# Normed input in two steps and one more block pair: a feed-forward change in a macaron block

## The chip, the cores and the metric

The kernel runs on one core of one Trainium2 chip. The metric is the device time of one execution in microseconds (us), the median of several runs. All times below are microseconds unless marked ns.

## The reference, cut to what matters

One layer: a half-weighted feed-forward network, a token mixer with two kinds of attention, a second half-weighted feed-forward network, and a last norm. There are 512 tokens of width 1024; the inner width of the feed-forward networks is 2816. All data are float32.

```python
def rmsnorm(x, g):
    y = x32 * lax.rsqrt(jnp.mean(x32 * x32, axis=-1, keepdims=True) + EPS)
    return (y * g.astype(jnp.float32)).astype(x.dtype)

def swiglu(x, w_gate, w_up, w_down):
    return (jax.nn.silu(x @ w_gate) * (x @ w_up)) @ w_down

x = x + 0.5 * swiglu(rmsnorm(x, ffn1_norm), ffn1_w_gate, ffn1_w_up, ffn1_w_down)
x = x + token_mixer(rmsnorm(x, mix_norm), ...)
x = x + 0.5 * swiglu(rmsnorm(x, ffn2_norm), ffn2_w_gate, ffn2_w_up, ffn2_w_down)
return rmsnorm(x, final_norm)
```

## The kernel before

Everything is held transposed: the width lies on the 128 partitions, so x is eight tiles `x[k]` of 128 x 512 (k = 0 to 7), and the inner width 2816 is 22 tiles j. [...] One product is three matmuls (`mm3`): high by high, high weight by low input, low weight by high input, at lines 98, 99 and 100. ScalarE makes the high part by a copy and VectorE the low part by a subtraction; for weights this is `split_w` (lines 89 and 90), on halves of a tile that the DMA queue of SP brings in, 512 KB each, three buffers deep (`raw`, `wh`, `wl`).

`ffn` runs once for each feed-forward network, with the names' suffix a or b; the text calls them layer one and layer two. It goes through the 22 tiles in three parts.

Plain tiles, j below `N0` = 6. Gate and up products use `eh` and `el`, the input times the norm's gain, but without the root mean square, which isn't known yet. 48 matmuls of 512 columns make a tile. While they run, `means` takes the column sums of the squares `sq` with four small matmuls and a chain of small VectorE operations (`rsqrt_steps`), and `spread` makes the factor `bc` for all partitions with one matmul and a copy into `rbc`. `hooks` says after which (j, k) each is called. `gate` then multiplies both results by `bc`, takes the Silu and the product, and `activated` splits the result into `ah` and `al` for the down projection: three multiplications and a subtraction on VectorE. In layer one the first two tiles are made together with the loading of x, so that its loop starts with j = 2.

Block pairs, j from 6 on, two tiles at a time, `pair`. The gate products of two tiles are made with seven block products instead of eight (Winograd's form of Strassen's scheme): on the weights' side with sums of weight blocks (`s1`, `s2`, and a difference in place of `raw`), on the input's side with four combinations t0 to t3 of the halves of two input tiles. This needs the normed input itself: `xh` and `xl`, and the combinations split as `th` and `tl`. The seven products are 84 matmuls of 256 columns; the two up products are plain, 24 matmuls of 512 columns each, and come after the gate products. The combinations of partial sums are taken out of PSUM between the products.

`normed(p)`, p = 0 to 3, prepares two input tiles each: the normed tiles `nx`, their parts `xh` and `xl`, the four combinations in two work tiles, and eight splits of 256 columns. It is called after (3, 3), (3, 7), (4, 3) and (4, 7).

Down projection: eight output tiles, 66 matmuls each.

TensorE's order is the order of the program (a manual schedule). The orders of VectorE and ScalarE in `ffn` are made by the scheduler of the language, from its own estimates, and are fixed in the program; each engine works them off in order, with semaphores between the engines. A weight split that stands behind other work on VectorE waits for it. PSUM has four banks for tiles of tag `mm` (plain tiles and pairs' gate products) and two of tag `t` (the pairs' up products). Work tiles of tags `ob` and `ptb` have two buffers each, and `slot` names 512-column places, in which the 22 tiles `ah` take slots 0 to 21.

Of the kernel before, what the change touches and what calls it, by code (L numbers as in the profile page):

```python
# [13 lines left out]
F32 = mybir.dt.float32  # L14
# [6 lines left out]
P = 128  # L21
# [14 lines left out]
WARM = 7  # L36
DIRECT = (0, 7)

N0 = 6
HS = S // 2  # L40
F32_MAX = 3.4028234e38
PSUM = bass.MemoryType.PSUM
# [5 lines left out]
def tile_macaron(ctx: ExitStack, tc, xs, xT, wf, wgu1, wst1, wd1, wqk, wv, wo, wgu2, wst2, wd2,  # L48
# [121 lines left out]

        return means, spread

    def ffn(wgu, wst, wd, norm, early, res, nm, hooks, first=None, last_halves=None):

# [1 line left out]

        eh, el = early
        ah, al, due = [None] * JF, [None] * JF, []  # L180
        th, tl = [], []

        def activated(j, t):
            h = ah[j] = slot(j, f"ah{nm}{j}", F32R)
# [2 lines left out]
            V.tensor_tensor(l[:], t[:], h[:].bitcast(F32), op=ALU.subtract)  # L187

        def gate(j, pg, pu):
            bc = res["bc"]  # L190
            t1 = tp.tile([P, S], F32, tag="ptb", name=f"t1{nm}{j}")
            V.tensor_tensor(t1[:], pg[:], bc[:], op=ALU.mult)
            A.activation(t1[:], t1[:], AF.Silu)
            t2 = tp.tile([P, S], F32, tag="ob", name=f"t2{nm}{j}")
            V.tensor_tensor(t2[:], pu[:], bc[:], op=ALU.mult)
            V.tensor_tensor(t2[:], t2[:], t1[:], op=ALU.mult)
            activated(j, t2)

        def t_tiles():
            tp.tile([P, 8], F32, tag="odd", name=f"odd{nm}", bufs=1)  # L200
            tiles = [tp.tile([P, 1280], F32R, tag=f"pr{i % 2}", name=f"tt{nm}{i}")
                     for i in range(4)]
            more = tp.tile([P, 12 * HS], F32R, tag="tx", name=f"tx{nm}", bufs=1)
            places = [t[:, i * HS:(i + 1) * HS] for t in tiles for i in range(5)]
            places += [more[:, i * HS:(i + 1) * HS] for i in range(12)]
            th.extend(places[4 * p:4 * p + 4] for p in range(4))
            tl.extend(places[16 + 4 * p:20 + 4 * p] for p in range(4))

        def normed(p):

            b = []
            for k in (2 * p, 2 * p + 1):
                t = tp.tile([P, S], F32, tag="ob", name=f"nx{nm}{k}")
                V.scalar_tensor_tensor(t[:], x[k], gain(norm, k), res["bc"][:],
                                       op0=ALU.mult, op1=ALU.mult)
                A.copy(xh[k][:], t[:])
                V.tensor_tensor(xl[k][:], t[:], xh[k][:].bitcast(F32), op=ALU.subtract)
                b += [t[:, :HS], t[:, HS:]]
            ta = tp.tile([P, S], F32, tag="ptb", name=f"ta{nm}{p}")
            tb = tp.tile([P, S], F32, tag="ptb", name=f"tb{nm}{p}")  # L220
            t1, t2, t3, t4 = ta[:, :HS], ta[:, HS:], tb[:, :HS], tb[:, HS:]
            V.tensor_tensor(t1, b[1], b[0], op=ALU.subtract)
            V.tensor_tensor(t2, b[3], t1, op=ALU.subtract)
            V.tensor_tensor(t3, b[3], b[1], op=ALU.subtract)
            V.tensor_tensor(t4, b[2], t2, op=ALU.subtract)
            for i, t in enumerate((t1, t2, t3, t4)):
                A.copy(th[p][i], t)
                V.tensor_tensor(tl[p][i], t, th[p][i].bitcast(F32), op=ALU.subtract)

        def block(k, half):  # L230
            c = slice(half * HS, (half + 1) * HS)
            return xh[k][:, c], xl[k][:, c]

        def pair(j):
            src = [wst[j + i - N0] for i in range(2)]
            (r0, h0, l0), (r1, h1, l1) = [load_w(src[i][0], f"sg{nm}{j + i}") for i in range(2)]
            u0, u1 = slice(0, 512), slice(512, 1024)
            h2, l2, h3, l3 = [wp.tile([P, 1024], F32R, tag=t, name=f"{t}_{i}{nm}{j}")
                              for i in (2, 3) for t in ("wh", "wl")]
            s1 = tp.tile([P, S], F32, tag="ob", name=f"s1{nm}{j}")  # L240
            s2 = tp.tile([P, S], F32, tag="ob", name=f"s2{nm}{j}")

            def split(t, h, l):
                A.copy(h, t)
                V.tensor_tensor(l, t, h.bitcast(F32), op=ALU.subtract)
# [24 lines left out]
            def t(i):  # L270
                return lambda p: (th[p][i], tl[p][i])
# [7 lines left out]
            product(pb, w2, t(1), True, True)  # L279
            V.tensor_tensor(w, pb, w, op=ALU.add)  # L280
            product(pc, w1, t(0), True, True)
            product(pd, w3, t(2), True, True)
# [4 lines left out]
            product(pd, a22, t(3), False, True)  # L287
            V.tensor_tensor(g1[:, left], pd, w, op=ALU.add)
            A.activation(g1[:], g1[:], AF.Silu)
            product(pc, w4, b(1, 1), False, True)  # L290
            V.tensor_tensor(g0[:, right], pc, w, op=ALU.add)
            A.activation(g0[:, right], g0[:, right], AF.Silu)
            for i, g in enumerate((g0, g1)):
                wh, wl = get_w(src[i][1], f"su{nm}{j + i}")
                pu = pp.tile([P, S], F32, tag="t", name=f"pu{nm}{j + i}", bufs=2)
                for k in range(KD):
                    o = slice(k * P, (k + 1) * P)
                    mm3(pu[:], wh[:, o], wl[:, o], xh[k][:], xl[k][:], k == 0, k == KD - 1)
                V.tensor_tensor(g[:], pu[:], g[:], op=ALU.mult)
                activated(j + i, g)  # L300

        j0 = 0
        if first is not None:
            j0 = 2
            due += first
        for j in range(j0, N0):
            if j == 2 and first is not None:
                pg, pu = [pp.tile([P, S], F32, tag="t", name=f"p{c}{nm}2", bufs=2) for c in "gu"]
            else:
# [2 lines left out]
            for hf in range(2):  # L312
                wh, wl = get_w(wgu[j, hf], f"gu{nm}{j}_{hf}")
                for kk in range(4):
                    k = hf * 4 + kk
                    for c, pt in ((0, pg), (1, pu)):
                        o = kk * 256 + c * P
                        mm3(pt[:], wh[:, o:o + P], wl[:, o:o + P], eh[k][:], el[k][:],
                            k == 0, k == KD - 1)
# [11 lines left out]
        for j in range(N0, JF, 2):  # L331
            pair(j)
        for m in range(KD):
            if m == 1 and "down" in hooks:
# [572 lines left out]

    n3 = {}
    means, spread = rstd("n3", n3)
    for m in ffn(wgu2, wst2, wd2, 2, early, n3, "b", {(0, 4): means, (0, 7): spread},  # L910
                 last_halves=last_halves):
        square_x(m)


# [88 lines left out]
```

## Time and profile before

| | |
|---|---|
| Median of 3 runs | 1009.64 (1009.6 to 1009.86) |
| The profiled execution, its own time | 1009.0 |
| Its span, first to last instruction | 1006.6 |
| Mean granted TensorE clock | 0.985 |
| PE (matmul) busy | 971.3 |
| DVE (VectorE) busy | 579.2 |
| ACT (ScalarE) busy | 425.1 |
| Plain tiles of layer one in the loop | 28.04 to 79.31 |
| Block pairs of layer one | 79.31 to 253.28 |
| Plain tiles of layer two | 620.72 to 698.32 |
| Block pairs of layer two | 698.32 to 873.30 |

PE, DVE, ACT, POOL and SP are TensorE, VectorE, ScalarE, GpSimd and the engine whose queue issues most DMAs; PEld is TensorE's loading of weights. The last four rows are start times of matmuls in the trace. The page shows the span in 40 equal slices of about 25 us, with the busy share of each slice in tenths. A wait line of the trace reads: who waited, its line, who released it; total, number of times and longest. Matmuls are pipelined: the time of one (0.39 for 512 columns) is longer than the distance between the starts of two (0.227), and the distance sets the pace.

### The profile page before, as it was taken

How to read it: one execution, taken by the hardware profiler on the slowest of the kernel's cores; microseconds unless marked ns; L12 is line 12 of the kernel's file. 1: busy time of each engine (PE TensorE's matmuls, PEld its weight loads, DVE VectorE, ACT ScalarE, POOL GpSimd, SP SyncE). 2: the span in 40 equal slices, each digit the busy share in tenths (PEclk: the TensorE clock that was granted, in tenths of full speed). 3: DMA queues.
4: the chain of work that ended last, by engine and by line, in shares of the span. 5: the costliest groups of instructions: out<-in, count | busy, mean ns of one | idle time of the engine just before them, and what ended most of it. 6: DMA issues, size and time to landing. Idle time of an engine off the chain costs nothing.

```text
span 1006.6 us, 13748 instructions
## 1 busy us (share of the span) xinstructions
PE 971.3 (96%) x5358; PEld 844.3 (84%) x5358; DVE 579.2 (58%) x1114; ACT 425.1 (42%) x792; POOL 32.4 (3%) x34
## 2 busy tenths in 40 slices
PE   9978999999999999999999999986999999999996
PEld 7867899988788888988989788875899889888886
DVE  6796666675332336669664455596666766422223
ACT  6453444434222235566756653353344344322230
POOL 0000000000001110000000013000000000000110
PEclk9998999999999999999999999998899999999998
DMA  7212223333233341444232113211233322433312
GB/s 248 88 45 102 84 85 126 102 108 109 91 100 94 95 152 63 126 127 122 87 115 76 63 45 123 97 50 43 85 125 105 105 85 90 130 100 94 94 58 84
DMA packets 32720, 98.71 MB, mean 98 GB/s; under 512 B 3776, under 2 KB 6080, under 8 KB 32656
## 3 DMA queue, kind: packets, MB, share of 16 engines
q1 hardware_dynamic: 32480, 97.55, 30.2%
q8 instruction: 42, 0.69, 0.3%
q0 software_dynamic: 176, 0.30, 0.2%
q14 instruction: 22, 0.18, 0.1%
HBM read 92.55 MB, written 2.14 MB: 94 GB/s over the span
## 4 chain that ended last, share of the span: by engine, by line
PE 88%; DVE 9%; issue 1%; ACT 1%; DMA 1%; SPq 0%; DVEq 0%; ACTq 0%
PE pda L98 4%; PE pda L100 4%; PE pda L99 4%; PE pub L98 4%; PE pub L99 4%; PE pub L100 4%; PE pua L99 4%; PE pua L98 4%; PE pua L100 4%; PE pdb L99 3%; PE pdb L98 3%; PE pdb L100 3%; PE po L672 2%; PE pwo L99 1%; PE pwo L98 1%; PE pwo L100 1%
## 5 line engine op out<-in xcount | busy, mean ns | idle before, releaser
L98 PE MATMUL pda<-aha,wh_da 128*128 128x512 f32 x176 | 68.6, 390 | 0.0
L100 PE MATMUL pda<-aha,wl_da 128*128 128x512 f32 x176 | 68.5, 389 | 0.0
L99 PE MATMUL pda<-ala,wh_da 128*128 128x512 f32 x176 | 68.5, 389 | 0.0
L90 DVE TENSOR_TENSOR wl_db<-raw_db,wh_db 128x1024 fp32r<-128x1024 f32 (+1 forms) x24 | 27.3, 1136 | 62.2 <-ACT wh_db L89 62.1
L90 DVE TENSOR_TENSOR wl_da<-raw_da,wh_da 128x1024 fp32r<-128x1024 f32 (+1 forms) x24 | 27.3, 1136 | 58.7 <-ACT wh_da L89 58.5
L89 ACT CAST wh_db<-raw_db 128x1024 fp32r<-128x1024 f32 (+1 forms) x24 | 23.6, 982 | 86.2 <-PE pdb L99 78.7
L98 PE MATMUL pdb<-ahb,wh_db 128*128 128x512 f32 x154 | 59.9, 389 | 0.0
L99 PE MATMUL pdb<-alb,wh_db 128*128 128x512 f32 x154 | 59.9, 389 | 0.0
L100 PE MATMUL pdb<-ahb,wl_db 128*128 128x512 f32 x154 | 59.9, 389 | 0.0
L89 ACT CAST wh_da<-raw_da 128x1024 fp32r<-128x1024 f32 (+1 forms) x24 | 23.5, 981 | 84.2 <-PE pda L99 55.5
L125 POOL TENSOR_TENSOR sq<-sq,sqt 128x512 f32<-128x512 f32 x20 | 28.7, 1437 | 680.6 <-ACT sqt L124 680.5
L638 DVE CUSTOM_DVE_ANT_0 pr<-sc,strip 128x128 f32<-128x128 f32 (+3 forms) x64 | 30.9, 489 | 34.1 <-PE sc L636 33.1
L98 PE MATMUL pua<-xh,wh_sua 128*128 128x512 f32 x128 | 49.9, 390 | 0.0
L98 PE MATMUL pub<-xh,wh_sub 128*128 128x512 f32 x128 | 49.9, 390 | 0.0
L99 PE MATMUL pub<-xl,wh_sub 128*128 128x512 f32 x128 | 49.9, 390 | 0.0
L99 PE MATMUL pua<-xl,wh_sua 128*128 128x512 f32 x128 | 49.9, 390 | 0.0
L100 PE MATMUL pua<-xh,wl_sua 128*128 128x512 f32 x128 | 49.8, 389 | 0.0
L100 PE MATMUL pub<-xh,wl_sub 128*128 128x512 f32 x128 | 49.8, 389 | 0.0
L641 ACT ACTIVATE pr<-pr,mx 128x128 f32<-128x128 f32 (+3 forms) x64 | 36.0, 563 | 30.8 <-DVE mx L638 29.8
L98 PEld LDWEIGHTS pda<-aha,wh_da 128*128 128x128 f32 x176 | 33.0, 188 | 7.3 <-ACT wh_da L89 0.5
L100 PEld LDWEIGHTS pda<-aha,wl_da 128*128 128x128 f32 x176 | 33.0, 188 | 6.9
L99 PEld LDWEIGHTS pda<-ala,wh_da 128*128 128x128 f32 x176 | 33.0, 188 | 6.9
(430 smaller groups left out, 2915.1 us busy)
## 6 DMA issues: line engine op xcount, KB each, us to landing
raw_sga<-wst_dram SPq DMA_DIRECT2D x16, 512.0 KB, 3.6
raw_sua<-wst_dram SPq DMA_DIRECT2D x16, 512.0 KB, 3.5
raw_da<-wd_dram SPq DMA_DIRECT2D x16, 512.0 KB, 3.5
raw_qk<-wqk_dram SPq DMA_DIRECT2D x16, 512.0 KB, 3.5
raw_sgb<-wst_dram SPq DMA_DIRECT2D x16, 512.0 KB, 4.2
raw_sub<-wst_dram SPq DMA_DIRECT2D x16, 512.0 KB, 3.5
raw_db<-wd_dram SPq DMA_DIRECT2D x16, 512.0 KB, 3.5
raw_gub<-wgu_dram SPq DMA_DIRECT2D x12, 512.0 KB, 3.5
```

The costliest lines, as they stand in the source:

```text
L89: A.copy(h[:, a:b], raw[:, a:b])
L90: V.tensor_tensor(l[:, a:b], raw[:, a:b], h[:, a:b].bitcast(F32), op=ALU.subtract)
L98: T.matmul(po, wh, mh, start=first, stop=False, skip_group_check=on)
L99: T.matmul(po, wh, ml, start=False, stop=False, skip_group_check=on)
L100: T.matmul(po, wl, mh, start=False, stop=last, skip_group_check=on)
L125: G.tensor_tensor(sq[:], sq[:], t[:], op=ALU.add)
L638: V.tensor_tensor_reduce(out=pi, in0=ps[:, :w], in1=st["b"][m][:, w - 1::-1], op0=ALU.add, op1=ALU.min, scale=1.0, scalar=3.0e38, accum_ou ...
L641: A.activation(pi, pi, AF.Exp, scale=-1.0, bias=st["mx"][:, m, i:i + 1], accum_out=st["ls"][:, m, i:i + 1])
L672: T.matmul(st["po3"][:, i, d0:d0 + dn], st["ptb", m, i][:, k * P:(k + 1) * P], vt[u // 4, k][:, fo + d0:fo + d0 + dn], start=k == 0, stop= ...
```

## The change

The constant `N0` gives way to two numbers for each layer: n0, the tiles on `eh` and `el`, and n1, where the pairs begin. Layer one has (5, 6): tile 5 stays plain, but reads the normed `xh` and `xl`. Layer two has (3, 4): tile 3 is plain on normed input, and tiles 4 and 5 become a pair.

The preparation is cut in two. `normed_x(p)` makes two normed tiles in slots 8 to 15, and their parts `xh` and `xl`; it is called after k = 1 and k = 5 of tiles n0 - 2 and n0 - 1. `normed_t(p)` makes the combinations in place in those slots and splits them, 512 columns at a time for p below 3; it is called after k = 3 and k = 7 of tile n0, and after k = 3 of the first pair's two up products. The first pair makes its up products ahead of its gate products. For tiles from n0 on, `gate` has no factor to apply: ScalarE takes the Silu straight from PSUM. In layer one `means` is called ahead of tile 2 instead of after its k = 0, and `spread` after k = 2 instead of k = 3. The host cuts the weights at the new n1.

```diff
-N0 = 6
+EARLY = (5, 3)
+PAIRED = (6, 4)
...
         def gate(j, pg, pu):
-            bc = res["bc"]
             t1 = tp.tile([P, S], F32, tag="ptb", name=f"t1{nm}{j}")
-            V.tensor_tensor(t1[:], pg[:], bc[:], op=ALU.mult)
-            A.activation(t1[:], t1[:], AF.Silu)
-            t2 = tp.tile([P, S], F32, tag="ob", name=f"t2{nm}{j}")
-            V.tensor_tensor(t2[:], pu[:], bc[:], op=ALU.mult)
-            V.tensor_tensor(t2[:], t2[:], t1[:], op=ALU.mult)
-            activated(j, t2)
+            if j < n0:
+                bc = res["bc"]
+                V.tensor_tensor(t1[:], pg[:], bc[:], op=ALU.mult)
+                A.activation(t1[:], t1[:], AF.Silu)
+                t2 = tp.tile([P, S], F32, tag="ob", name=f"t2{nm}{j}")
+                V.tensor_tensor(t2[:], pu[:], bc[:], op=ALU.mult)
+                V.tensor_tensor(t1[:], t2[:], t1[:], op=ALU.mult)
+            else:
+                A.activation(t1[:], pg[:], AF.Silu)
+                V.tensor_tensor(t1[:], pu[:], t1[:], op=ALU.mult)
+            activated(j, t1)
...
+        def normed_x(p):
+            for k in (2 * p, 2 * p + 1):
+                n = slot(8 + k, f"nx{nm}{k}")
+                nx.append(n)
+                V.scalar_tensor_tensor(n[:], x[k], gain(norm, k), res["bc"][:],
+                                       op0=ALU.mult, op1=ALU.mult)
+                A.copy(xh[k][:], n[:])
+                V.tensor_tensor(xl[k][:], n[:], xh[k][:].bitcast(F32), op=ALU.subtract)
...
+        def normed_t(p):
+            if p == 0:
+                t_places()
+            t0, t1 = nx[2 * p], nx[2 * p + 1]
+            u0, u1 = slice(0, HS), slice(HS, S)
+            V.tensor_tensor(t0[:, u0], t0[:, u1], t0[:, u0], op=ALU.subtract)
+            V.tensor_tensor(t0[:, u1], t1[:, u1], t0[:, u1], op=ALU.subtract)
+            V.tensor_tensor(t1[:, u1], t1[:, u1], t0[:, u0], op=ALU.subtract)
+            V.tensor_tensor(t1[:, u0], t1[:, u0], t1[:, u1], op=ALU.subtract)
+            for i, t in enumerate((t0, t1)):
+                c = slice(i * S, (i + 1) * S)
+                if p < 3:
+                    A.copy(th[p][:, c], t[:])
+                    V.tensor_tensor(tl[p][:, c], t[:], th[p][:, c].bitcast(F32), op=ALU.subtract)
+                else:
+                    for q, u in enumerate((u0, u1)):
+                        h = th[p][2 * i + q]
+                        A.copy(h, t[:, u])
+                        V.tensor_tensor(tl[p][:, i * S + q * HS:i * S + (q + 1) * HS], t[:, u],
+                                        h.bitcast(F32), op=ALU.subtract)
...
         def pair(j):
-            src = [wst[j + i - N0] for i in range(2)]
+            src = [wst[j + i - n1] for i in range(2)]
+            ups = [up(j + i, src[i][1]) for i in range(2)] if j == n1 else []
...
             for i, g in enumerate((g0, g1)):
-                wh, wl = get_w(src[i][1], f"su{nm}{j + i}")
...
+                pu = ups[i] if ups else up(j + i, src[i][1])
                 V.tensor_tensor(g[:], pu[:], g[:], op=ALU.mult)
                 activated(j + i, g)
+
+        def up(j, src):
+            wh, wl = get_w(src, f"su{nm}{j}")
+            pu = pp.tile([P, S], F32, tag="t", name=f"pu{nm}{j}", bufs=2)
+            for k in range(KD):
+                o = slice(k * P, (k + 1) * P)
+                mm3(pu[:], wh[:, o], wl[:, o], xh[k][:], xl[k][:], k == 0, k == KD - 1)
+                prepared(j, k)
+            return pu
...
+        prepare = {(n0 - 2 + p // 2, 1 + p % 2 * 4): (normed_x, p) for p in range(4)}
+        prepare.update({(n0, 3): (normed_t, 0), (n0, 7): (normed_t, 1),
+                        (n0 + 1, 3): (normed_t, 2), (n0 + 2, 3): (normed_t, 3)})
...
-        for j in range(j0, N0):
+        for j in range(j0, n1):
+            mv = (eh, el) if j < n0 else (xh, xl)
...
-                    if j in (3, 4) and k % 4 == 3:
-                        if not th:
-                            t_tiles()
-                        normed((j - 3) * 2 + k // 4)
+                    prepared(j, k)
...
-    for m in ffn(wgu1, wst1, wd1, 0, early, n1, "a",
-                 {(2, 0): means, (2, 3): spread, "down": bias_rows}, firsts):
+    means()
+    for m in ffn(wgu1, wst1, wd1, EARLY[0], PAIRED[0], 0, early, n1, "a",
+                 {(2, 2): spread, "down": bias_rows}, firsts):
```

More of the change, by code (lines that the diff above doesn't have):

```diff
@@ L171, in rstd, with ffn @@
         return means, spread
-    def ffn(wgu, wst, wd, norm, early, res, nm, hooks, first=None, last_halves=None):
+    def ffn(wgu, wst, wd, n0, n1, norm, early, res, nm, hooks, first=None, last_halves=None):
         eh, el = early
         ah, al, due = [None] * JF, [None] * JF, []
-        th, tl = [], []
+        nx, th, tl = [], [], []
         def activated(j, t):
@@ L200, in t_tiles, with t_places @@
+            activated(j, t1)
[7 more added lines that the diff above has]
+                V.tensor_tensor(xl[k][:], n[:], xh[k][:].bitcast(F32), op=ALU.subtract)
+        def t_places():
             tp.tile([P, 8], F32, tag="odd", name=f"odd{nm}", bufs=1)
-            tiles = [tp.tile([P, 1280], F32R, tag=f"pr{i % 2}", name=f"tt{nm}{i}")
-                     for i in range(4)]
+            rows = [tp.tile([P, 5 * HS], F32R, tag=f"pr{p % 2}", name=f"tt{nm}{p}")
+                    for p in range(4)]
@@ L203, in t_tiles @@
             more = tp.tile([P, 12 * HS], F32R, tag="tx", name=f"tx{nm}", bufs=1)
[L204 to L228, printed above, removed]
@@ new lines, in t_places @@
+            tl.extend(t[:, :4 * HS] for t in rows)
+            th.extend(more[:, 4 * p * HS:4 * (p + 1) * HS] for p in range(3))
+            th.append([t[:, 4 * HS:] for t in rows])
+        def normed_t(p):
[18 more added lines that the diff above has]
+                                        h.bitcast(F32), op=ALU.subtract)
@@ L278, in pair @@
             A.copy(w, pa)
-            product(pb, w2, t(1), True, True)
+            product(pb, w2, t(3), True, True)
             V.tensor_tensor(w, pb, w, op=ALU.add)
             product(pc, w1, t(0), True, True)
-            product(pd, w3, t(2), True, True)
+            product(pd, w3, t(1), True, True)
             V.tensor_tensor(g1[:, right], pd, w, op=ALU.add)
@@ L286, in pair @@
             A.activation(g0[:, left], pa, AF.Silu)
-            product(pd, a22, t(3), False, True)
+            product(pd, a22, t(2), False, True)
             V.tensor_tensor(g1[:, left], pd, w, op=ALU.add)
@@ L293, in pair @@
             for i, g in enumerate((g0, g1)):
-                wh, wl = get_w(src[i][1], f"su{nm}{j + i}")
[L295 to L298, printed above, removed]
+                pu = ups[i] if ups else up(j + i, src[i][1])
                 V.tensor_tensor(g[:], pu[:], g[:], op=ALU.mult)
                 activated(j + i, g)
+        def up(j, src):
[6 more added lines that the diff above has]
+            return pu
         j0 = 0
@@ L330, in ffn @@
                 gate(*due.pop(0))
-        for j in range(N0, JF, 2):
+        for j in range(n1, JF, 2):
             pair(j)
@@ L909, in tile_macaron @@
     means, spread = rstd("n3", n3)
-    for m in ffn(wgu2, wst2, wd2, 2, early, n3, "b", {(0, 4): means, (0, 7): spread},
-                 last_halves=last_halves):
+    for m in ffn(wgu2, wst2, wd2, EARLY[1], PAIRED[1], 2, early, n3, "b",
+                 {(0, 4): means, (0, 7): spread}, last_halves=last_halves):
         square_x(m)
@@ L955, in col_tiles, with block_tiles @@
         return np.ascontiguousarray(a(w).reshape(k, P, n, P).transpose(2, 1, 0, 3)).reshape(n, P, k * P)
-    def block_tiles(g, u):
-        g, u = [col_tiles(t)[N0:].reshape(JF - N0, P, KD, P) for t in (g, u)]
+    def block_tiles(g, u, n):
+        g, u = [col_tiles(t)[n:].reshape(JF - n, P, KD, P) for t in (g, u)]
         g = np.concatenate([g[:, :, 0::2], g[:, :, 1::2]], axis=2)
-        return np.ascontiguousarray(np.stack([g, u], axis=1)).reshape(JF - N0, 2, P, KD * P)
+        return np.ascontiguousarray(np.stack([g, u], axis=1)).reshape(JF - n, 2, P, KD * P)
     wi = a(w_in[0])
```

18 lines of the change are left out of this document (11 added, 7 removed).

## The prediction, made before the changed kernel ran

> **What bounds the kernel now.** I read the page first, then the PE's waits, then busy time by stretch, then the start times of single instructions.
>
> The page: the kernel is TensorE work with few holes, at two places.
>
> ```profile
> PE 971.3 (96%) x5358; PEld 844.3 (84%) x5358; DVE 579.2 (58%) x1114; ACT 425.1 (42%) x792; POOL 32.4 (3%) x34
> PE   9978999999999999999999999986999999999996
> DVE  6796666675332336669664455596666766422223
> PEclk9998999999999999999999999998899999999998
> ```
>
> The second and fourth rows dip at slices 2 to 3 (50 to 100 us) and 26 to 28 (654 to 730 us). VectorE's row reads 9 at both. These are the stretches in which each feed-forward layer prepares the operands of its first pair. The PE's waits name what is missing:
>
> ```profile
> PE pgb L100 <- DVE wl_gub L90: 7.5, 2, 4.4
> PE pga L100 <- DVE wl_gua L90: 5.3, 2, 3.3
> PE pxa L98 <- ACT wh_sga L244: 4.3, 1, 4.3
> PE pxb L98 <- ACT wh_sgb L244: 4.3, 1, 4.3
> PE pxa L100 <- DVE wl_sga L245: 0.4, 1, 0.4
> PE pxb L100 <- DVE wl_sgb L245: 0.4, 1, 0.4
> ```
>
> Six waits, 22.2 us, all for split weights of the two layers. The weights had landed; the splits stood behind other work on VectorE (the ScalarE ones wait for sums made on VectorE). By stretch, in the second layer (PE, PEld, DVE, ACT, POOL, PEclk):
>
> ```profile
> 632.00:643.00 11.00, 11.00 (x49) 8.72 (x48) 5.63 (x7) 4.53 (x5) 0.00 (x0) 1.00 0.21 66
> 643.00:654.00 11.00, 11.00 (x50) 9.13 (x49) 5.13 (x6) 3.26 (x4) 0.00 (x0) 1.00 0.29 99
> 654.00:665.00 11.00, 11.00 (x51) 9.09 (x50) 10.22 (x20) 6.24 (x11) 0.00 (x0) 1.00 0.21 75
> 665.00:676.00 11.00, 7.97 (x36) 6.28 (x35) 11.00 (x24) 6.53 (x12) 0.00 (x0) 1.00 0.00 0
> 676.00:690.00 14.00, 9.57 (x33) 7.43 (x32) 12.24 (x25) 5.58 (x12) 0.00 (x0) 0.78 0.31 103
> ```
>
> VectorE is half idle for 22 us after the spread sums are there, then full for 34 us, and the PE starves; the clock then falls to half for 6.8 us at a time (matmuls 0.425 apart instead of 0.227 after 685.35). VectorE's prices, start to start, stand in one excerpt of its timeline:
>
> ```profile
> 656.03 0.74 DVE L214 SCALAR_TENSOR_TENSOR nxb<-x,rbc_n 128x512 f32<-128x512 f32 x1
> 656.69 1.22 DVE L90 TENSOR_TENSOR wl_gub<-raw_gub,wh_gub 128x1024 fp32r<-128x1024 f32 x1
> 657.83 0.69 DVE L196 TENSOR_TENSOR t2b<-t2b,t1b 128x512 f32<-128x512 f32 x1
> 658.43 0.69 DVE L217 TENSOR_TENSOR xl<-nxb,xh 128x512 fp32r<-128x512 f32 x1
> 659.03 0.42 DVE L222 TENSOR_TENSOR tab<-nxb 128x256 f32<-128x256 f32 x1
> 659.37 0.69 DVE L187 TENSOR_TENSOR alb<-t2b,ahb 128x512 fp32r<-128x512 f32 x1
> ```
>
> So 0.66 for a normed row tile, 1.14 for a 1024-wide split, 0.60 for 512 wide, 0.335 for 256 wide.
>
> **What the two transitions cost.** 48 matmuls of a plain tile take 10.88 (642.08 to 652.96 in layer two). Two tiles with sums and spread take 23.62 there (620.72 to 644.34), so sums and spread cost 1.86. Layer one: tile 2 starts at 28.04, the first pair at 79.31: 51.27 - 4 x 10.88 - 1.86 = 5.89 lost. Layer two: 620.72 to 698.32 is 77.60 - 6 x 10.88 - 1.86 = 10.46 lost. A steady pair takes 20.87 (748.06 to 768.93); the first ones take 27.86 (79.31 to 107.17) and 28.86 (698.32 to 727.18): 6.99 and 7.99 lost. Together 31.33 us: the 22.2 of waits, and 9.1 of slow clock and restarts.
>
> [...]
>
> **The change, part by part.**
>
> *Normed input early (layer two).* The eight normed tiles with their high and low parts move from tiles 3 and 4 to tiles 1 and 2, into VectorE's idle half, and the transforms to tile 3 and the first pair's up products. In the order of the changed kernel all eight normed steps stand before the last split of tile 3. VectorE's work from the spread copy (634.79, unmoved) to the last split needed for the first three products is then: 5 wide splits 5.70; 8 normed 5.28; spread copy, 14 gate operations, 8 xl, 6 wide lows of transforms and 7 of the pair's first splits and sums, 36 x 0.60 = 21.60; 20 narrow ones 6.70; 39.3 in all, done by about 674.1, with 0.7 more for chained operations 674.8. The PE has 620.72 + 1.86 + 4 x 10.88 + two up products 10.91 = 677.0 until the first product. Slack 2.2: the three waits go. If VectorE were later, each microsecond would be a microsecond of PE.
>
> *Layer one.* Its plain tiles stay four, the last on normed input, with two gate operations instead of four. From the spread copy: 7 wide splits 7.98, 8 normed 5.28, 44 x 0.60 = 26.40, 20 narrow 6.70: 46.4. The copy starts at about 34.9 (below), and VectorE idles about 1.6 for the first Silu, whose table load (1.28 in the trace) stands behind a weight cast; chained operations add 0.6: end at 83.5. The PE reaches the first product at 28.04 + 1.86 + 0.75 + 43.52 + 10.91 = 85.1. Slack 1.6; again the three waits go. The tightest place inside is tile 3's second weight half: its split stands behind tile 2's gate, ends near 46.9, and is wanted at 47.4. I take nothing; bounds 0 and 1.
>
> *Sums and spread of layer one.* The sums go ahead of tile 2 (sq was complete at 22.6, the PE arrives at 28.04: no wait). The spread is now one k earlier, and a 1.14 split has slipped into the chain of small operations. That chain took 3.54 (30.38 to 33.92); 29.0 + 3.54 + 1.14 = 33.7, while the PE is through three k at 28.04 + 0.81 + 18 x 0.2267 = 32.9. The PE waits about 0.75 (0.4 to 1.2), with the rest of tile 2 behind it: +0.75.
>
> *Up products first.* The same instructions in another order; on SP's queue two weight loads pass two others (512 KB, 3.5 us to landing, buffers three deep). Two pairs' gate products now follow each other without 10.9 us of up products between, so the first pair's evacuations and the next pair's splits meet on VectorE. Before, no such meeting exists; the nearest row is the 0.4 wait of the first product. I take 0.3 per layer, bounds 0 and 1.5.
>
> *One more pair in layer two.* 84 + 48 matmuls replace 96: 2 x 10.88 - 20.87 = 0.89 gained. Four 512 KB loads replace four.
>
> *Gate on normed tiles, places of the transforms, eight slots.* Two VectorE operations fewer, ScalarE reads PSUM directly (nearest row: the 256-wide copy from PSUM, 0.36 against 0.40 from SBUF), 512-wide lows instead of two narrow ones (0.60 against 0.67). All inside the sums above. The slots' former readers end at 620.9 or before 22.6, long before the first normed tile. Cost nothing; if a buffer were late, it would show as a VectorE wait inside the slack.
>
> Sum: 31.33 + 0.89 - 0.75 - 0.6 = 30.9. The profiled execution took 1009.0 (span 1006.6, 2.4 around it): 978.1, span 975.7. The median of the runs lies 0.6 above the profiled one: 978.8.
>
> **Rivals.** *A wait stays.* One of the slacks (0.5, 1.6, 2.2) is too thin and one or two of the PE's holes come back, by the rows 2 to 4.4 idle and 2.4 to 3.4 of slow clock if over about 4: 2 to 8 us, 981 to 987. For: three margins under 2.3 us. Against: prices are the same in busy and quiet stretches. *Slow clock anyway.* The half-rate spells come without the long waits: 8.4 back, 987. Against: all three began in or just after waits over 4 us, none after the 3.0 and 3.3 ones. *Not what it says.* The normed work still ends late: only 0.9 gained and 0.75 lost, about 1009.5; against it stands the order of instructions. *Slower.* VectorE's price per operation rises, because working in place in the eight slots, with ScalarE busy on the same tiles beside it, costs more than the present buffers do. Its 86 us of work in the two stretches has 3.8 us of slack; beyond that each microsecond is a PE wait, with up to 8.4 of slow clock on top. Slower than before from 86 + 3.8 + 22.5 on, that is 30% (0.60 becoming 0.78); at 35% it gives about 1013. Nothing in the rows shows such a spread: 0.60 stands in every stretch.
>
> **Numbers.** Forecast 0.80, a wait stays 0.12, slow clock 0.03, not what it says 0.02, slower 0.03. The forecast's own bounds: spread 0.4 to 1.2, meeting 0 to 3.0 for both layers, tile 3 up to 1: from 977.4 with none of them to 982.3 with all, and 0.9 below for the offset between profile and median (0.6) and its scatter. Range 976.5 to 986, which reaches into the first rival and leaves out some 0.1. About 0.2% (2 us) is what a measurement can tell from no change: faster 0.95, same 0.02, slower 0.03.
>
> **What would show it.** In the profile after: none of the six waits above; a granted clock of 1.00 through both transitions; VectorE busy near 9 or more of 11 us in the two quiet stretches of layer two; 36 matmuls more; a spread wait of under 1.2 in layer one; layer one shorter by about 12 and layer two by about 19. It would be wrong if the PE waited over 2 us for any split weight, or if 512-wide VectorE operations were no longer 0.60 apart.

## The result, and the profile after

The changed kernel takes 977.08 us (976.96 to 977.1, four runs); the kernel before took 1009.75 in the four runs beside it (1009.6 to 1012.51). The ratio is 0.967, with a 95% interval of 0.9653 to 0.9687. Against the median that the prediction started from this is 0.967 x 1009.64 = 976.3. The forecast was 978.8, with a range from 976.5. The mechanism came as described, but the gain was larger than forecast, by 1.7 in the runs themselves and by 2.5 in the ratio, and by the ratio the time lies 0.2 below the range. The profiled execution took 977.07, its span is 974.8, its mean granted clock 0.997 (before 0.985).

The page of the changed kernel, the rows that answer to those of before:

```profile
PE 961.4 (99%) x5394; PEld 839.6 (86%) x5394; DVE 577.6 (59%) x1108; ACT 426.0 (44%) x787; POOL 32.4 (3%) x34
PE   9999999999999999999999999999999999999996
DVE  7698767765232336668764546797677566422223
PEclk9999999999999999999999999999999999999998
```

The PE has 36 matmuls more and is busy 9.9 us less, mainly because none of its matmuls in the two layers runs at half rate (the granted clock is 1.00 from 6.2 to 968.8). Both dips are gone from PE's row and from the clock's. VectorE does the same amount of work (577.6 against 579.2); slice 25, in layer two's plain tiles, now reads 7 where it read 5.

All lines of the PE's waits that belong to the two feed-forward layers (who waited, its line, who released it: total, times, longest):

```profile
PE bc_n L169 <- DVE dg_n L165: 0.5, 1, 0.5
...
PE pzb L100 <- DVE g1b L301: 0.3, 1, 0.3
PE pza L100 <- DVE g1a L301: 0.2, 1, 0.2
```

The waits for split weights are gone. (The prediction calls them six; its six lines hold eight waits, 22.2 us, and the six long ones are 21.4 of them.) Three others are left, 1.0 together: the spread that comes one k too early, and in each layer the sixth product of the first pair, which waits until VectorE has taken that pair's fourth product out of the same PSUM bank.

Busy time by stretch in layer two (PE, PEld, DVE, ACT, POOL, PEclk), which now begins at 608.3:

```profile
620.00:631.00 11.00, 11.00 (x48) 8.76 (x47) 9.69 (x15) 7.23 (x10) 0.00 (x0) 1.00 0.17 48
631.00:642.00 11.00, 11.00 (x50) 9.09 (x50) 11.00 (x17) 5.24 (x8) 0.00 (x0) 1.00 0.31 93
642.00:653.00 11.00, 11.00 (x50) 9.13 (x49) 11.00 (x23) 6.47 (x10) 0.00 (x0) 1.00 0.39 116
653.00:664.00 11.00, 11.00 (x50) 9.09 (x50) 9.64 (x19) 4.91 (x10) 0.00 (x0) 1.00 0.08 31
```

Before, the two stretches after the spread had VectorE busy for 5.63 and 5.13 of 11 us, and two stretches later the PE was busy for 7.97. Now VectorE is at 9.6 to 11 from the start, and the PE has no hole. The margin can be read where the first pair begins. The last of that pair's first four splits, from VectorE's timeline, and the first gate product, from PE's:

```profile
661.39 0.68 DVE L262 TENSOR_TENSOR wl_sgb<-raw_sgb,wh_sgb 128x512 fp32r<-128x512 f32 x1
```

```profile
664.60 0.28 PE L100 MATMUL pwb<-xh,wh_sgb 128*128 128x256 f32 x1
```

The split ends at 662.07, 2.5 us ahead. Counted from the start of layer two that is 53.7 and 56.3; the forecast had 54.1 and 56.3. The room is larger than that, because this split is for the fourth product, which begins at 668.87. The split with the least room is that of the second product, with its first matmul:

```profile
660.78 0.68 DVE L262 TENSOR_TENSOR wl_sgb<-s2b,wh_sgb 128x512 fp32r<-128x512 f32 x1
```

```profile
666.04 0.28 PE L100 MATMUL pxb<-txb,wh_sgb 128*128 128x256 f32 x1
```

It ends at 661.46, 4.6 us ahead.

Where the time went, by the first matmul of each stage (profiled executions):

| Stage | before | after | difference | forecast |
|---|---|---|---|---|
| up to tile 2 of layer one (after: to the sums ahead of it) | 28.04 | 27.37 | -0.67 | 0 |
| layer one, its loop | 225.24 | 213.52 | -11.72 | -11.8 |
| down projection of layer one and token mixer | 367.45 | 367.45 | 0 | 0 |
| layer two, its loop | 252.57 | 233.79 | -18.79 | -19.0 |
| down projection of layer two, seven of eight tiles | 104.72 | 104.72 | 0 | 0 |
| last output tile and last norm | 28.54 | 27.94 | -0.61 | 0 |

### The profile page after: what moved, and what is told of

It reads as the page before. It is cut to its first block, busy times and chain, and to the rows that moved or that the text cites. A ratio compares the mean times of both kernels' runs of the same rounds, so it can differ in the third digit from the quotient of the medians.

```text
span 974.8 us, 13809 instructions
## 1 busy us (share of the span) xinstructions
PE 961.4 (99%) x5394; PEld 839.6 (86%) x5394; DVE 577.6 (59%) x1108; ACT 426.0 (44%) x787; POOL 32.4 (3%) x34
## 4 chain that ended last, share of the span: by engine, by line
PE 94%; DVE 3%; ACT 1%; DMA 1%; issue 1%; DVEq 0%; POOL 0%; ACTq 0%; POOLq 0%
PE pda L100 4%; PE pub L100 4%; PE pub L101 4%; PE pda L102 4%; PE pda L101 4%; PE pub L102 4%; PE pua L100 4%; PE pua L101 4%; PE pua L102 4%; PE pdb L101 4%; PE pdb L100 4%; PE pdb L102 4%; PE po L704 2%; PE pwo L100 1%; PE pwo L101 1%; PE pwo L102 1%
## 5 line engine op out<-in xcount | busy, mean ns | idle before, releaser
L92 DVE TENSOR_TENSOR wl_da<-raw_da,wh_da 128x1024 fp32r<-128x1024 f32 (+1 forms) x24 | 27.2, 1135 | 58.7 <-ACT wh_da L91 58.6
L100 PE MATMUL pub<-xh,wh_sub 128*128 128x512 f32 x144 | 56.1, 390 | 0.0
L101 PE MATMUL pub<-xl,wh_sub 128*128 128x512 f32 x144 | 56.1, 390 | 0.0
L102 PE MATMUL pub<-xh,wl_sub 128*128 128x512 f32 x144 | 56.0, 389 | 0.0
```

Of the source, the lines that this page charges most:

```text
L92: V.tensor_tensor(l[:, a:b], raw[:, a:b], h[:, a:b].bitcast(F32), op=ALU.subtract)
L100: T.matmul(po, wh, mh, start=first, stop=False, skip_group_check=on)
L101: T.matmul(po, wh, ml, start=False, stop=False, skip_group_check=on)
L102: T.matmul(po, wl, mh, start=False, stop=last, skip_group_check=on)
```

## Experiments

The theory to be tested: the PE loses time only where a weight split on VectorE, which works its list off in order, comes later than the PE. The change cures this by three things together, that is normed steps in VectorE's idle half, transforms apart from them so that the plain tiles' weight splits are not queued behind both, and 10.9 us of up products as cover for the first pair's splits. One rival is that one of these alone would do; another, that the slow clock and not the waits is what matters.

### The same two kernels again

No edit; both kernels were run again, the one before three times with a profile. Expected of the kernel before:

> The kernel before, once more, for the two stretches that the change does not touch. In the first two profiles the tile after the loading stretch starts at 28.04 (before) and its place at 27.37 (after), and from the last output tile's first product to the end it is 28.55 against 27.94: 1.27 us that the prediction had at nothing. Theory A, these belong to the single execution (when a load lands, where the clock's half-rate spells fall): this profile shows other values than 28.04 and 28.55, by some tenths. Theory B, they belong to the kernel: 28.04 and 28.55 again within 0.05. In both the two layers cost 225.2 and 252.6 from tile start to down projection, and the six waits are 22.2 in all.

> The kernel before once more. Its times in three sessions run from 1008.2 to 1014.6, those of the changed kernel from 976.9 to 978.3. [...] Rival (the waits vary from one execution to the next): the spells are the same, the waits differ by several microseconds.

> [...]

and of the changed one:

> The changed kernel again, beside the three variants below, on one chip. In all profiles so far the start of the loading stretch and the end move by up to 0.8 and 0.6 from one execution to the next, with the clock's half-rate spells; the changed kernel has one spell only, in the end. Theory (its waits are all under 0.5 us, so that no spell falls into its layers): 976 to 978 in every run, within 0.8 of each other, while the kernel before spreads over several microseconds. Rival (977.1 was one lucky state of the clock): some runs 2 or more above.

Measured: 1008.37, 1013.96 and 1010.02 for before; 977.03 for the changed kernel (976.92 to 978.34, four runs), whose two layers take 213.38 and 233.47. One of its four runs, 978.34, lies outside the 0.8 that was expected; none lies 2 above, as the rival had it. The kernel before ran 24 times in all, from 1008.2 to 1014.6. The forms of the changed kernel below that have no wait for weights stay between 976.6 and 978.4. So most of the spread belongs to the kernel before. Its waits hardly move: those for split weights are 21.2 to 22.2 in the four profiles. What moves is the clock. In the execution of the prediction, after the wait of 3.03 at the second half of a plain tile's weights, matmuls follow each other at 0.23 (PE's timeline):

```profile
675.19 0.50 PE L100 MATMUL pgb<-ehb,wl_gub 128*128 128x512 f32 x1 [3.03 <-DVE wl_gub L90]
...
676.46 0.39 PE L99 MATMUL pgb<-elb,wh_gub 128*128 128x512 f32 x1
676.68 0.39 PE L100 MATMUL pgb<-ehb,wl_gub 128*128 128x512 f32 x1
```

In the run of 1008.37 the same wait, of the same length, is followed by a half-rate spell from 676.1 to 679.5:

```profile
674.55 0.50 PE L100 MATMUL pgb<-ehb,wl_gub 128*128 128x512 f32 x1 [3.03 <-DVE wl_gub L90]
...
676.45 0.63 PE L98 MATMUL pub<-ehb,wh_gub 128*128 128x512 f32 x1
676.88 0.63 PE L99 MATMUL pub<-elb,wh_gub 128*128 128x512 f32 x1
```

The starts are 0.43 apart instead of 0.23. The spells in the two transitions were three of 6.83 in the prediction's execution; three of 3.41 and one of 6.83 in the run of 1008.37; two of 3.41 and four of 6.83 in that of 1013.96, where one came after the 2.0 us wait at 58.8; one of 3.41 and three of 6.83 in that of 1010.02. Layer one takes 225.06 to 230.07 accordingly, layer two 252.6 to 253.6. So the slow clock is not a fixed property of this kernel: waits of 2 to 4.4 us start it or don't, for 3.41 or 6.83 us.

Of the two theories for the stretches outside the layers each is right for one: the start moves from execution to execution, the end is 28.54 to 28.56 in all four.

### The waits filled

On the kernel before, small matmuls on a constant tile were put where the PE stands still, into a bank of their own; nothing reads them.

```diff
+        def fill(n, at):
+            ps = pp.tile([P, S], F32, tag="s", name=f"fill{nm}{at}", bufs=2)
+            for i in range(n):
+                T.matmul(ps[:, :P], ones_m[:], ones_m[:], start=True, stop=True)
+        fills = {("a", 4, 4): 7, ("a", 5, 4): 12, ("b", 4, 4): 12, ("b", 5, 0): 17}
...
+                    if (nm, j, k) in fills:
+                        fill(fills[nm, j, k], f"{j}_{k}")
...
+            if j == N0:
+                fill(18, "p")
```

> The kernel before, with small matmuls on constants (128 columns, into a spare bank, never read) ahead of each of the six waits, 7 to 18 of them, so that TensorE works where it waited; VectorE's work and order are the same. Theory (the long waits let the clock fall to half, and those spells cost 8.4 in the first profile and other amounts in other executions, which is why the kernel before spreads from 1008.2 to 1014.6): no spell in the two layers, layer one near 222.9 and layer two near 246.5, in all about 1000, and the runs within about 1 of each other. Rival (the waits are all, and the spells do not matter): 1008 to 1014, with the same spread. Rival (the filling delays the real work): slower than before.

Measured: 1001.79 (1001.17 to 1002.08, four runs) against 1010.84 (1008.28 to 1014.2, seven); ratio 0.9907 (0.9878 to 0.9935). The granted clock is 1.00 through both transitions. The end of a wait in PE's timeline:

```profile
678.39 3.96 PE L307 MATMUL fillb<-ones_m 128*128 128x128 f32 x34
683.41 0.50 PE L100 MATMUL pgb<-ehb,wl_gub 128*128 128x512 f32 x1 [0.60 <-DVE wl_gub L90]
```

The fills end short of the splits, so they delay nothing, and the splits still come late. What is gained is the slow clock alone: 9.1 by the medians, 7.4 against the profiled execution (1009.0 to 1001.59). Layer one falls by 1.6 and layer two by 5.0 against that execution, 6.6 together, where the prediction had put 8.4 on the clock. Part of the 1.8 between them is that a wait behind a spell is shorter: the second wait of layer two's plain tiles is 3.8 in the two executions in which a spell came between it and the first (1008.37, 1013.96), and 4.4 in the two in which none did. Counted from the end of the first wait, the PE reached the second one 1.6 and 2.8 later in these two than in the prediction's execution, but the split came only 1.0 and 2.1 later. The rest of the 1.8 is not accounted for. The spread of the runs falls from 5.9 to 0.9. The rival that the clock is what matters falls: 25 of some 34 us remain, for the waits and what hangs on them.

### Up products first, alone

The kernel before, with its first pair's up products moved ahead; the preparation as it was.

```diff
+            ups = [up(j + i, src[i][1]) for i in range(2)] if j == N0 else []
...
+                pu = ups[i] if ups else up(j + i, src[i][1])
```

> The kernel before with one part of the change: the first pair's up products come first; normed input in one step, pairs from tile 6, as before. Theory (the PE loses time only where a split on VectorE is later than the PE): the first pair's 6.99 and 7.99 go, since 10.9 us of up products stand ahead; the waits of the plain tiles (5.89 and 10.46) stay, as their splits stand behind the same work. About 14 us faster than before, 995 to 996. Rival (order of work alone is the whole gain): near 978. Rival (early normed input is the whole gain, up products only swap places): near 1009.

Measured: 998.34 (two runs, 998.19 and 998.48); ratio 0.9862 (0.9779 to 0.9944). That misses the expectation by some 2.5. The interval is wide, here and in the next two experiments, since the three runs of the kernel before beside them lie at 1008.22, 1014.22 and 1014.6; the parts are therefore compared by stage. Its waits:

```profile
PE pgb L100 <- DVE wl_gub L90: 7.3, 2, 4.2
PE pga L100 <- DVE wl_gua L90: 5.5, 2, 3.5
```

The first pairs' waits are gone, and the loss of the first pairs falls from 7.0 and 8.0 to under 0.2. But the plain tiles now lose 8.6 and 12.3 instead of 5.9 and 10.5, with waits as before: the spells of half rate lie wholly within them here (6.83 at 72.5, 6.83 at 669.9, 3.41 at 683.5). The expectation had held the plain tiles' loss fixed; it is a loss of waits and of a clock that falls where it will. As for the theory: by the two layers' loops this part alone brings 10.1 of the 30.5 us, a third.

### One step early

On top of the last one: `normed`, still in one step with its transforms, is called in tiles 1 and 2 of layer two.

```diff
+        n_at = 3 if nm == "a" else 1
...
-                    if j in (3, 4) and k % 4 == 3:
+                    if j in (n_at, n_at + 1) and k % 4 == 3:
...
-                        normed((j - 3) * 2 + k // 4)
+                        normed((j - n_at) * 2 + k // 4)
```

> As e1_up_first_alone, and in layer two the old one-step preparation, with its two-buffered work tiles, called after tiles 1 and 2 instead of 3 and 4. Rival (all that counts is that the preparation starts in VectorE's idle time): layer two's 10.5 us of waits go too, about 985. Theory (the place of the splits in VectorE's order counts; in one step 41 us of transforms, sums and normed tiles for four p stand ahead of the weight splits of tile 3, which two steps leave until tile 3 is on its way): the waits move to tile 3's weights, and part of the gain only is had, 988 to 994.

Measured: 992.22 (992.18 and 992.26); ratio 0.9801 (0.9719 to 0.9883). Layer two takes 241.83 instead of 246.57, and not the 233.5 of the changed kernel. One long wait is left in it, at the second weight half of tile 3. VectorE's timeline ahead of it, and the matmul that waits:

```profile
657.66 0.75 DVE L228 TENSOR_TENSOR txb<-tbb,ttb 128x256 fp32r<-128x256 f32 x2
...
658.93 0.68 DVE L195 TENSOR_TENSOR t2b<-pub,rbc_n 128x512 f32<-128x512 f32 x1
659.53 1.22 DVE L90 TENSOR_TENSOR wl_gub<-raw_gub,wh_gub 128x1024 fp32r<-128x1024 f32 x1
```

```profile
660.80 0.80 PE L100 MATMUL pgb<-ehb,wl_gub 128*128 128x512 f32 x1 [4.68 <-DVE wl_gub L90]
```

The split stands behind the transforms and a gate. This is the case for two steps: the transforms aren't wanted before the first gate products, and in one step they hold up the splits of tiles that come earlier. Time alone, VectorE's idle half, isn't enough; the order in its queue is what counts. This form still differs from the changed kernel in more than the two steps: the changed kernel also has normed tiles in slots of their own, wider splits and a shorter gate. No run separates these.

### Up products last

The changed kernel, with the first pair's up products after its gate products, as before; the transforms are called earlier, in tile n0, since the pair has no up products ahead of it to hold them.

```diff
-            ups = [up(j + i, src[i][1]) for i in range(2)] if j == n1 else []
+            ups = []
...
-        prepare.update({(n0, 3): (normed_t, 0), (n0, 7): (normed_t, 1),
-                        (n0 + 1, 3): (normed_t, 2), (n0 + 2, 3): (normed_t, 3)})
+        prepare.update({(n0, 1 + 2 * p): (normed_t, p) for p in range(4)})
```

> The changed kernel with the first pair's up products after its gate products again; the transforms for all four p are called during tile n0. Theory: the PE comes to the first product 10.9 us earlier. In the changed kernel's profile the splits that the second product needs end 4.0 us (layer two: 661.5 against 666.0) and 3.8 us (layer one) ahead; 10.9 less that and less the two splits for the up products (2.3) that may now come later gives waits of about 4.7 per layer, with up to 3.4 of slow clock each: 8 to 16 slower than the changed kernel, 985 to 993. Rival (VectorE is no longer the limit after the normed input moved): 977 to 978.

Measured: 987.65 (986.39 and 988.91); ratio 0.9756 (0.9669 to 0.9843). Layer one is 3.8 longer than in the changed kernel, layer two 6.0. Its waits:

```profile
PE pwb L102 <- DVE wl_sgb L262: 1.5, 1, 1.5
PE pxa L100 <- ACT wh_sga L261: 1.4, 1, 1.4
PE pxb L100 <- ACT wh_sgb L261: 1.4, 1, 1.4
...
PE pga L102 <- DVE wl_gua L92: 1.0, 1, 1.0
```

About 3 of waits come back in each layer, where 4.7 had been forecast, and in layer two a spell of 6.83 at half rate, most of it on matmuls (some 3 lost). So the cover of 10.9 in each layer is worth about 10 in both together. The 1.0 is in a plain tile of layer one, whose split stands behind transforms (67.59 and 68.19 in VectorE's timeline), which were called earlier as well. Up products first can't be left out, then, nor, in layer two, the second step with what goes with it. No run leaves out the early normed steps alone, so whether they are needed is not shown.

### Extra work on VectorE

The changed kernel, with each wide low part of layer two's transforms computed twice (6 operations more, 3.6 us) or five times (24 more, 14.4 us; the 1 in the diff is then a 4).

```diff
-                    V.tensor_tensor(tl[p][:, c], t[:], th[p][:, c].bitcast(F32), op=ALU.subtract)
+                    for _ in range(1 + (1 if nm == "b" else 0)):
+                        V.tensor_tensor(tl[p][:, c], t[:], th[p][:, c].bitcast(F32), op=ALU.subtract)
```

> The changed kernel with ballast: in layer two the six 512-wide low parts of the transforms are computed twice, six more VectorE operations, 3.6 us, between the spread and the first pair. Theory (VectorE has room there: in the changed kernel's profile the splits for the second product end 4.0 us before the PE wants them, those for the up products 2.7 or more): no difference to c_after within 0.3. Rival (VectorE is at its limit and each microsecond counts): 3 to 4 slower, more with a slow clock.

> The changed kernel with four times the ballast of e5_ballast_6: in layer two each of the six low parts of the transforms is computed five times, 24 more VectorE operations of 0.60, 14.4 us. Theory (VectorE has about 4 us of room in layer two, and each microsecond beyond is a wait of the PE): the PE waits about 10 in all, for the up products' and the first pair's splits, plus up to 3.4 of slow clock for each wait over some 3.4: 10 to 17 slower, 987 to 994. Rival (the room is larger than 14 us, VectorE is not the limit): 977.

Measured: with 6, 977.11 (976.99 to 977.51) beside 977.03 without, layer two 233.50 against 233.47: no difference. With 24, 988.67 (988.38 and 988.96), layer two 244.46, that is 11.0 more. Its waits:

```profile
PE pwb L102 <- DVE wl_sgb L263: 4.5, 1, 4.5
PE pub L102 <- DVE wl_sub L92: 2.7, 1, 2.7
```

7.2 is waits, where about 10 had been expected; most of the rest is one half-rate spell of 6.83, of which 1.5 lies inside the second wait. That a spell takes a wait of over some 3.4 is shown by no run: one began 1.5 after a wait of 1.99 (the run of 1013.96), one in a wait of 3.03 (up products first, alone), and none followed the wait of 3.26 in the prediction's execution. Of the extra 14.4, then, 7.2 was covered. That is more than the 2.2 of the prediction and the 4 of the two expectations. The two waits say why: they are for the second up product and for the first gate product, and that product's own split ends 6.5 ahead of its use in the changed kernel (658.34 and 664.84), not 2.5. (Their 4.0, from 661.5 and 666.0, should read 4.5.) Beyond the cover the PE waits for VectorE, as the rival of a dearer VectorE had it.

### Layer two cut like layer one

```diff
-EARLY = (5, 3)
-PAIRED = (6, 4)
+EARLY = (5, 5)
+PAIRED = (6, 6)
```

> The changed kernel with layer two cut as layer one is: five tiles on early input, one plain on normed input, pairs from tile 6. The ninth pair is undone, all else stays. Theory (a pair costs 20.87 against 21.76 of two plain tiles, and nothing waits in either): 0.9 slower than c_after. Rival (the ninth pair matters because it brings VectorE's work forward, or costs splits): over 2 slower, or faster.

Measured: 978.09 (977.97 to 978.4), 1.06 more than the changed kernel beside it; layer two 234.55, 1.08 more. The ninth pair was forecast at 0.89. With eight pairs in layer two there are again 5358 matmuls, and still no wait for a split weight: the extra pair is a small gain beside the rearrangement, not its source.

The run shows one thing more. With n0 = 5 the program calls `normed_x` in tiles 3 and 4 of layer two again, two k ahead of the old places. Yet VectorE starts the first normed tile 16.0 us after the layer's first matmul (608.40), as it does in the changed kernel, and not 35.3 as before:

```profile
624.39 0.74 DVE L210 SCALAR_TENSOR_TENSOR nxb<-x,rbc_n 128x512 f32<-128x512 f32 x1
```

So it wasn't the place of the call that brought the normed steps into VectorE's idle half, but the order that the scheduler made. That it could bring them forward because the normed tiles have slots of their own, in place of the two-buffered `ob` tiles that the gates use too, is likely; no run shows it.

### The spread of layer one after k = 3

```diff
-                 {(2, 2): spread, "down": bias_rows}, firsts):
+                 {(2, 3): spread, "down": bias_rows}, firsts):
```

> The changed kernel with layer one's spread after k = 3 of tile 2, as before, instead of k = 2; the sums still come ahead of tile 2. Theory (the 0.49 wait of the spread matmul, 0.73 with restart against 1.86 of an undisturbed one, has no cover at k = 2): the wait goes, and the split of tile 3's second half, 0.4 ahead of the PE in the profile, is about 0.6 later; 0.2 to 0.7 faster than c_after, or equal where the split now waits. Rival (the early spread is needed): over 0.5 slower.

Measured: 977.35 (976.63 to 977.88), beside 977.03: inconclusive by the runs. In the trace the wait of the spread is gone and layer one takes 212.73, 0.65 less. Its tail is 28.46 against 27.94, which takes most of that back. By the stages it is the best version of all; that it is faster isn't shown.

## Where the prediction was right, and which of its steps failed

The mechanism and the two layers' sums held. What failed is what the sum started from: one execution of the kernel before, taken for its fixed time, with nothing for the start and the end and 0.3 for scatter.

*The six waits go, with what hangs on them (31.33).* Right. Layer one was to lose 11.83 (5.89 + 6.99, less 0.75 and 0.3) and lost 11.72; layer two 19.04 (10.46 + 7.99 + 0.89 - 0.3) and lost 18.79. The three slacks in which the prediction saw its risk held: 2.5 for 2.2 in layer two, 1.8 for 1.6 in layer one (82.6 and 84.4), and the thinnest, tile 3's second weight half in layer one, 0.4 for 0.5. The first two are too strict: the prediction counts seven sums and splits to the last one "needed for the first three products", but the seventh is the fourth product's, and the sum sets them all against the start of the first. VectorE's prices did not move, in place or not: 0.60 for 512 columns, 0.335 for 256.

*The spread, +0.75.* Right: the wait is 0.49, and with the restart it is 0.73.

*The meeting of first and second pair, 0.3 each.* Too small: the first two pairs' gate products, 168 matmuls, take 20.39 in layer one and 20.51 in layer two, where two steady ones take 2 x 9.97. That is 0.45 and 0.57, inside the bounds of 0 and 1.5. All of it falls on the first pair; the second one takes 9.97 in both layers. The first pair's sum L301 (VectorE's timeline) stands behind the sums for the second pair's weights, and the first pair's sixth product (PE's) waits for it:

```profile
671.11 0.68 DVE L270 TENSOR_TENSOR raw_sgb<-raw_sgb,raw_sgb 128x512 f32<-128x512 f32 x1
671.71 0.42 DVE L301 TENSOR_TENSOR g1b<-pzb,sq 128x256 f32<-128x256 f32 x1
```

```profile
672.18 0.39 PE L100 MATMUL pzb<-txb,wh_2b 128*128 128x256 f32 x1 [0.31 <-DVE g1b L301]
```

*Start and end at nothing.* This step failed: 0.67 and 0.61 were gained there, although the change touches neither. The profile that the sum started from had drawn a long start and a long end. The start takes 27.1 to 28.0 in the four profiles of the kernel before, and 27.2 to 27.8 in those of the changed kernel and its variants. In the prediction's execution the first matmul of the loading of x waited 0.57 for a weight copy; in the one after it did not. The tail takes 27.9 or 28.0 in some executions and 28.3 to 28.6 in others. It depends on whether the last spread matmul falls into a spell of half rate. Before, it did, with the spell from 997.8 on (PE's timeline):

```profile
998.98 1.22 PE L880 MATMUL bcl<-dgl,ones_m 128*128 128x256 f32 x2 [1.73 <-DVE dgl L876]
```

After, the same matmul ran at 967.73 and the spell began at 968.8, just behind it. The wait is the same, 1.72, and the matmul takes 0.70 instead of 1.22. All four profiles of the kernel before have 28.54 to 28.56 there, but variants of the changed kernel have 28.45 too (6 operations more, eight pairs), so the changed kernel doesn't always gain it: part of the 0.61 is luck.

*The offset, +0.6.* This step failed too. The profiled execution of the changed kernel (977.07) is at its median (977.08). The 0.6 of before lies within the scatter of a kernel whose clock falls differently in each execution, and was carried over as if it were fixed. Start, end, offset and what the two layers fell short give 0.67 + 0.61 + 0.6 - 0.1 - 0.25 = 1.5 of the 1.7 between forecast and measurement; 0.1 of the rest lies around the span (2.4 before, 2.3 after).

*The clock, "none after the 3.0 and 3.3 ones", and three spells of 6.8.* Read from one execution and taken for a property of the kernel. This is the step behind a range that was too narrow at its low end: it allowed 0.3 for scatter, but the median of before was itself a draw out of 1008.2 to 1014.6. Against 977.1 the gain is 31 to 37.5, depending on the execution of the kernel before that one takes. Of the four runs beside the changed kernel one was 1012.51, which puts their mean at 1010.4 and the ratio below the range. (The upper bound of the sum, 982.3, adds up to 982.6; nothing hangs on it.)

The 8.4 that the rivals put on the slow clock stands in the profiled execution: of its three spells of 6.83, the parts from 85.18, 685.35 and 704.21 on fall on matmuls, 4.6, 5.2 and 6.8 us, and half of that is 8.3. For the sum of that one execution it was the right figure. What it could not show is that the sum differs from run to run: the spells are 3.41 or 6.83 long, and the same wait of 3.03 is followed by one in one execution and not in another. What sets their length and their moment is not shown.

*Rivals.* No wait stayed, and in the two layers the slow clock did not come without waits (granted clock 1.00 in both). The mechanism of the rival "a wait stays" is real: three of the experiments, each without a part of the change, have such waits, at 987.7 to 998.3, and so has the one with too much work on VectorE. The price rise of the rival "slower" never came. What it would do is shown by the extra work in layer two: 3.6 us cost nothing, 14.4 cost 11.0, of which 7.2 is waits.

## What to carry to other kernels

Where a busy engine waits on an in-order one that is half idle on the average, look at the stretch before the wait: early idle time is worth something only if what is moved there doesn't stand ahead of work that is wanted sooner, so cut a preparation at the point where its parts have different due times, and put independent work ahead of the first user. Where a scheduler makes the order, read from the trace where the work landed: the place of the call need not be its place in the queue. When a kernel before has waits that let the clock fall, its own time is a distribution (1008.2 to 1014.6 here): take several profiles of it before a forecast to 0.2%, and put its scatter into the range. Stages that an edit doesn't touch still differ between two profiles, here by 0.67 and 0.61; compare them by stage before the difference is put down to the edit.

## What the runs showed of the hardware that was not expected

The same wait of 3.03 us is followed by full rate in one execution (matmuls 0.23 apart) and by half rate in another (0.43), and a wait of 1.99 us was followed by it in one; each spell inside the layers lasts 3.41 or 6.83 us. Small matmuls in the waits kept the granted clock at full rate (1.00) through both transitions and took 9.1 us off by the medians, without making any operand come sooner. A slow spell ahead of a wait cost less than the time it took from the matmuls: the wait behind it was 3.8 instead of 4.4 us.
